# One transformer layer on one core: the split products stream their moving operand and their result from the last column to the first

## The chip, the cores and the metric

The kernel runs on one core of a Trainium2 chip. The metric is the device time of one execution in microseconds. Before the change the median of three runs is 1590.91 us, the lowest 1588.34 and the highest 1592.03. The profile shows one further execution of 1586.72 us, whose span from the first to the last instruction is 1585.0 us.

## The reference

The layer takes x of 512 tokens by 1024 in float32. Cut to what matters here:

```
h    = rms_norm(x)
proj = h @ w_in                       # 1024 x 3328
A, B, M = stick-breaking attention, gated recurrence, attention into 256 memory tokens
x    = x + concat(A, B, M) @ w_out    # 1024 x 1024
h2   = rms_norm(x)
q    = h2 @ w_query                   # 1024 x 2048, then the 16 best of 128 keys, twice, in 8 heads
act  = gelu(h2 . expert_u[idx])       # 16384 experts of 1024 numbers
x    = x + sum(gate * act * expert_v[idx])
```

All large products are float32 in the reference.

## The kernel before

The engines are TensorE (PE, with its weight load PEld), VectorE (DVE), ScalarE (ACT), GpSimd (POOL) and SyncE (SP). The order of the work is laid down by a planner: the stages are generators, the class `Pace` holds an estimated clock for each engine, and the class `Threads` always continues the stage whose estimated time is smallest. Each call goes through one recording helper, line 204, so nearly every row of the profile has the line L204, and groups are told apart by tiles.

A float32 product is made of three products in the type float32r. Each operand is split in a high part and a low part, and high by high, low by high and high by low are added up in one bank of PSUM. The helper `mm3` (line 417) issues these three. A stationary operand always is 128 by 128; the moving operand is 256, 384 or 512 columns wide, and each product has a weight load of its own.

The stages that call `mm3`, with the tile that the profile names as the result:

- `proj_t` (line 497): projections with tokens on partitions, 256 columns, tile `pt` in the input projection and the memory keys, `qp` in a part of the query projection (`query`, line 1037).
- `outproj` (line 961): the output projection, 256 columns, tile `op`.
- `query` (line 1101): the rest of the query projection, 384 columns, tile `qf`.
- `dense`: for three of the four blocks of 128 tokens every expert is computed. `u_mm` (line 1394) makes the 128 blocks of `expert_u`, with 24 products of 384 columns each, tile `ua`; `v_mm` (line 1469) makes the 128 blocks of `expert_v`, with 18 products of 512 columns each into six banks that stay open to the end, tile `pin`.

Not through `mm3` go the other part of the input projection (`proj_f`, line 484, tile `pf`, the same three products written out by hand), the recurrence (`hs` and others, plain float32), the attention scores (`sz`), and the sums of one-hot rows (`gsum`, line 1267, tile `gb`, float16, whose operands are read with a step of two elements).

The fourth block of tokens fetches its expert rows one by one with indirect DMAs of POOL, and VectorE multiplies them, beside `dense`. Results of PE are read by ACT or DVE in their usual order of columns; these reads are not in the diff.

Of the kernel before, what the change touches and what calls it, by code (L numbers as in the profile page):

```python
# [264 lines left out]
def tile_trunk_layer(ctx: ExitStack, tc: tile.TileContext, x, mem, w_in, w_kv, w_out, w_query,  # L265
# [43 lines left out]
    def f(ap):  # L309
        return ap.bitcast(F32)  # L310


    xs = [page([P, D], name="x") for _ in range(NT)]
    mt = [page([P, D], name="mem") for _ in range(2)]
# [100 lines left out]
            return (a, b), (c, d)  # L415

    def mm3(o, lh, ll, rh, rl, first, last):
        PE.matmul(o, lh, rh, start=first, stop=False)
        PE.matmul(o, lh, rl, start=False, stop=False)
        PE.matmul(o, ll, rh, start=False, stop=last)  # L420
# [76 lines left out]
    def proj_t(W, t, o, xh, xl):  # L497
        hi, lo = W
        for k in range(KD):
            a, c = t * P, t * P + P  # L500
            mm3(o, hsl(xh, k, a, c), hsl(xl, k, a, c), hi[k // 4][:, k % 4], lo[k // 4][:, k % 4],
                k == 0, k == KD - 1)
# [458 lines left out]
    def outproj(ts):  # L961
        yield f"mix{ts[0]}"
        xr, ob = {}, {}
        for c in range(4):
            hi, lo = ws.get()
            for t in ts:
                if th.later(f"mix{t}"):
                    yield f"mix{t}"
                if t not in xr:
                    xr[t] = page([P, D], name="xr")  # L970
                    SP.dma_start(xr[t], x[t * P:(t + 1) * P])
                if c % 2 == 0:
                    ob[t] = bank("op")
                mh, ml = mix[t]
                for k in range(KD):
                    mm3(ob[t][:, (c % 2) * 256:(c % 2) * 256 + 256], mh[:, k], ml[:, k],
                        hi[k // 4][:, k % 4], lo[k // 4][:, k % 4], k == 0, k == KD - 1)
                if c % 2:
                    yield "pe"
                    cs = slice((c // 2) * 512, (c // 2) * 512 + 512)  # L980
                    V.tensor_tensor(xr[t][:, cs], xr[t][:, cs], ob[t], op=OP.add)
                if c == 3:
                    th.add(norm2(t, xr[t]), at=pace.unit_v + ND2)
            yield "pe"
# [52 lines left out]
    def query(ts, todo):  # L1037
# [49 lines left out]
        for n, h in enumerate(todo):  # L1087
# [8 lines left out]
            if ts is DENSE and n >= QF:  # L1096
                for c in range(2):
                    b = bank("qf")
                    for k in range(KD):
                        w, lw = [x[k // 4][:, k % 4, c * P:(c + 1) * P] for x in W]  # L1100
                        mm3(b[:, :TD], w, lw, hsl(h2hi, k, 0, TD), hsl(h2lo, k, 0, TD), k == 0, k == KD - 1)
                    qT = t2([P, TD], name="qT")
                    A.activation(qT, b[:, :TD], AF.Copy)
                    if pend2:
                        tail2()
                    if pend:
                        tail()
                    elif len(pendf) > 1:
                        tailf()
                    pendf.append(qT)  # L1110
                    yield
                continue
# [555 lines left out]
```

## Time and profile before

| what | value |
|---|---|
| median of three runs | 1590.91 us |
| profiled execution | 1586.72 us |
| its span | 1585.0 us |
| PE busy | 1557.2 us, 98% |
| PEld busy | 1424.2 us, 90% |
| DVE busy | 1267.9 us, 80% |
| ACT busy | 749.5 us, 47% |
| POOL busy | 353.2 us, 22% |
| mean granted TensorE clock | 0.995 of 2.4 GHz |
| DMA | 422.72 MB, mean 267 GB/s |

A row of matmuls gives the length of each from its start to its modelled end. Matmuls are pipelined, so the next starts long before that end; what one costs in a dense stretch is the distance from start to start. Rows of a timeline give the start, then the length, both in us.

### The profile page before, as it was taken

The page shows a single profiled execution, that of the slowest core. Times are in us where ns is not written, and L with a number is a line of the kernel's source. Part 1 is how long each engine was busy: PE and PEld are TensorE (multiplying, and loading weights), DVE is VectorE, ACT ScalarE, POOL GpSimd, SP SyncE. Part 2 cuts the span into 40 slices and gives each one's busy share as a digit, 9 for nine tenths or more (in the row PEclk, how much of TensorE's full clock was granted, in tenths as well). Part 3 has the DMA queues.
Part 4 walks back from the last instruction along what each step waited for, and adds up shares of the span by engine and source line. Part 5 has one row for each costly group of instructions (what it writes and reads, how often), then busy time and mean ns, then how long its engine had stood idle before and what let it go on. Part 6 is the DMA issues. An engine that isn't in the chain of part 4 may idle for free.

```text
span 1585.0 us, 25696 instructions
## 1 busy us (share of the span) xinstructions
PE 1557.2 (98%) x9367; PEld 1424.2 (90%) x9367; DVE 1267.9 (80%) x2536; ACT 749.5 (47%) x1428; POOL 353.2 (22%) x340
## 2 busy tenths in 40 slices
PE   8999999989999999999999999999999999999998
PEld 6998988888999999999999999988888888888887
DVE  5475669786788888788877878768889888888886
ACT  6331268844443455666566755433333333333332
POOL 3000000000061212112211111134344444344430
PEclk9999999989999999999999999999999999999999
DMA  6322203353397878889879888899999999999991
GB/s 253 107 81 80 70 12 107 129 191 121 110 332 262 263 237 291 277 298 309 264 270 302 273 295 275 284 408 408 408 407 408 398 377 383 394 386 377 368 378 75
DMA packets 163951, 422.72 MB, mean 267 GB/s; under 512 B 13552, under 2 KB 62704, under 8 KB 163824
## 3 DMA queue, kind: packets, MB, share of 16 engines
q1 hardware_dynamic: 67824, 236.51, 40.9%
q0 software_dynamic: 36864, 134.23, 23.0%
q10 hardware_dynamic: 59136, 50.34, 9.9%
q8 instruction: 73, 1.20, 0.3%
q14 instruction: 54, 0.44, 0.1%
HBM read 366.50 MB, written 54.53 MB: 266 GB/s over the span
## 4 chain that ended last, share of the span: by engine, by line
PE 95%; DVE 2%; ACT 2%; DMA 0%; issue 0%; SPq 0%; ACTq 0%; DVEq 0%
PE ua L204 34%; PE pin L204 33%; PE pf L204 6%; PE pt L204 4%; PE qf L204 4%; PE gb L204 3%; PE op L204 3%; PE sz L204 2%; PE hs L204 2%; PE qp L204 1%; PE so L204 1%; PE qs L204 1%; DVE tka L204 1%; ACT se L204 1%; DMA w<-in_w_in_dram 0%; PE mo L204 0%
## 5 line engine op out<-in xcount | busy, mean ns | idle before, releaser
L204 DVE TENSOR_TENSOR xlo<-ex,xhi 128x1024 fp32r<-128x1024 f32 x256 | 312.5, 1221 | 99.3 <-issue 46.3
L204 POOL DMA_INDIRECT row<-in_u_rows_dram,eidx x128 | 157.8, 1233 | 924.1 <-DVE tka L204 424.5
L204 PE MATMUL ua<-h2hi,xhi 128*128 128x384 f32 x1024 | 349.1, 341 | 0.0
L204 PE MATMUL ua<-h2hi,xlo 128*128 128x384 f32 x1024 | 342.9, 335 | 0.0
L204 PE MATMUL ua<-h2lo,xhi 128*128 128x384 f32 x1024 | 342.6, 335 | 0.0
L204 ACT ACTIVATE whi<-w 128x384 fp32r<-128x384 f32 (+1 forms) x202 | 142.6, 720 | 372.9 <-DVE w L204 325.1
L204 PE MATMUL pin<-xhi,whi 128*128 128x512 f32 x768 | 299.6, 390 | 1.5 <-ACT whi L204 1.5
L204 PE MATMUL pin<-xlo,whi 128*128 128x512 f32 x768 | 299.6, 390 | 1.2 <-DVE xlo L204 1.2
L204 PE MATMUL pin<-xhi,wlo 128*128 128x512 f32 x768 | 299.3, 390 | 0.0
L204 ACT ACTIVATE xhi<-ex 128x1024 fp32r<-128x1024 f32 x256 | 268.7, 1051 | 25.4 <-ACT stg L204 8.3
L204 POOL DMA_INDIRECT row<-in_v_rows_dram,eidx x128 | 178.3, 1393 | 253.1 <-DVE w L204 129.5
L204 DVE TENSOR_TENSOR wlo<-w,whi 128x384 fp32r<-128x384 f32 (+1 forms) x200 | 156.2, 795 | 90.5 <-PE pin L204 50.1
L204 PEld LDWEIGHTS ua<-h2lo,xhi 128*128 128x128 f32 x1024 | 192.5, 188 | 0.0
L204 PEld LDWEIGHTS ua<-h2hi,xhi 128*128 128x128 f32 x1024 | 192.2, 188 | 0.2
L204 PEld LDWEIGHTS ua<-h2hi,xlo 128*128 128x128 f32 x1024 | 192.2, 188 | 0.0
L204 PEld LDWEIGHTS pin<-xhi,whi 128*128 128x128 f32 x768 | 144.4, 188 | 31.9 <-ACT whi L204 1.8
L204 PEld LDWEIGHTS pin<-xlo,whi 128*128 128x128 f32 x768 | 144.6, 188 | 31.7 <-DVE xlo L204 1.5
L204 PEld LDWEIGHTS pin<-xhi,wlo 128*128 128x128 f32 x768 | 144.6, 188 | 30.0
L204 DVE SCALAR_TENSOR_TENSOR xg<-row,rsb,xg 128x1024 f32<-128x1024 f32 x128 | 163.7, 1279 | 0.9
L204 DVE CUSTOM_DVE_ANT_0 row<-row,xr 128x1024 f32<-128x1024 f32 x128 | 155.0, 1216 | 4.3 <-DMA row<-in_u_rows_dram,eidx 4.3
L204 ACT ACTIVATE gel<-ua 128x384 f32<-128x384 f32 x128 | 62.8, 491 | 190.0 <-PE ua L204 188.3
L204 ACT ACTIVATE oh<-oh,gpg 128x128 f16<-128x128 f16 x256 | 84.3, 436 | 16.3 <-DVE rsb L204 3.8
(262 smaller groups left out, 2283.7 us busy)
## 6 DMA issues: line engine op xcount, KB each, us to landing
ex<-in_u_t_dram SPq DMA_DIRECT2D x128, 512.0 KB
ex<-in_v_rows_dram SPq DMA_DIRECT2D x128, 512.0 KB
gel<-gel ACTq DMA_DIRECT2D x64, 384.0 KB
gd<-stg ACTq DMA_DIRECT2D x48, 512.0 KB
G<-gd SPq DMA_DIRECT2D x48, 512.0 KB
gel<-gel SPq DMA_DIRECT2D x64, 384.0 KB
w<-in_w_query_dram SPq DMA_DIRECT2D x28, 512.0 KB
w<-in_w_in_dram SPq DMA_DIRECT2D x26, 512.0 KB
```

The costliest lines, as they stand in the source:

```text
L204: r = fn(*args, **kw)
```

## The change

A helper `back` turns an access pattern round in all its free dimensions: the offset moves to the last element, and each step changes its sign. `mm3` applies it to the result in PSUM and to both parts of the moving operand, so that column n of the operand still goes to column n of the result, in descending order of n. The stationary operands stay as they are. The diff in full:

```diff
@@ -309,6 +309,15 @@
     def f(ap):
         return ap.bitcast(F32)
 
+    def back(ap):
+
+        d = [list(x) for x in ap.ap]
+        off = ap.offset
+        for a in range(1, len(d)):
+            off += d[a][0] * (d[a][1] - 1)
+            d[a][0] = -d[a][0]
+        return type(ap)(ap.tensor, off, d)
+
@@ -415,6 +424,7 @@
             return (a, b), (c, d)
 
     def mm3(o, lh, ll, rh, rl, first, last):
+        o, rh, rl = back(o), back(rh), back(rl)
         PE.matmul(o, lh, rh, start=first, stop=False)
         PE.matmul(o, lh, rl, start=False, stop=False)
         PE.matmul(o, ll, rh, start=False, stop=last)
```

On every engine the same instructions stand in the same order. What differs is on PE alone: some matmuls carry other waits. The first place is in the middle of the blocks of `expert_u`, where each first product into a new bank, `ua`, follows the last product of the block before it:

```order
 L204 MATMUL ua_5711<-h2lo_4067,xhi_5594 128x384
 L204 MATMUL ua_5711<-h2hi_4066,xlo_5634 128x384
-L204 MATMUL ua_5753<-h2hi_4060,xhi_5632 128x384 [waits Activation_49]
+L204 MATMUL ua_5753<-h2hi_4060,xhi_5632 128x384 [waits PE_49,Activation_49]
 L204 MATMUL ua_5753<-h2lo_4061,xhi_5632 128x384
 L204 MATMUL ua_5753<-h2hi_4060,xlo_5671 128x384 [waits DVE_49]
```

Nothing moved; the first product of the bank also waits for an earlier matmul of PE. The second place is the start of the `expert_v` blocks, the first product into each of the banks 2 to 6 of `pin`:

```order
 L204 MATMUL pin_11811<-xhi_11726,wlo_11799 128x512
-L204 MATMUL pin_11812<-xhi_11726,whi_11797 128x512
+L204 MATMUL pin_11812<-xhi_11726,whi_11797 128x512 [waits PE_49]
 L204 MATMUL pin_11812<-xlo_11801,whi_11797 128x512
 L204 MATMUL pin_11812<-xhi_11726,wlo_11799 128x512
-L204 MATMUL pin_11813<-xhi_11726,whi_11797 128x512
+L204 MATMUL pin_11813<-xhi_11726,whi_11797 128x512 [waits PE_49]
```

Here too the order is kept, and the first product of each bank carries a wait for PE that it did not have. Over the whole program the waits of PE for PE are 204 before and 334 now.

## Rows read from the trace of the kernel before

**Rows 1.** The page's parts 1 and 2: busy time, and 40 slices.

```profile
span 1585.0 us, 25696 instructions
PE 1557.2 (98%) x9367; PEld 1424.2 (90%) x9367; DVE 1267.9 (80%) x2536; ACT 749.5 (47%) x1428; POOL 353.2 (22%) x340
...
PE   8999999989999999999999999999999999999998
...
PEclk9999999989999999999999999999999999999999
```

**Rows 2.** The chain that ended last: shares by engine, then by line.

```profile
PE 95%; DVE 2%; ACT 2%; DMA 0%; issue 0%; SPq 0%; ACTq 0%; DVEq 0%
PE ua L204 34%; PE pin L204 33%; PE pf L204 6%; PE pt L204 4%; PE qf L204 4%; PE gb L204 3%; PE op L204 3%; PE sz L204 2%; PE hs L204 2%; PE qp L204 1%; PE so L204 1%; PE qs L204 1%; DVE tka L204 1%; ACT se L204 1%; DMA w<-in_w_in_dram 0%; PE mo L204 0%
```

**Rows 3.** Waits of PE, longest and shortest of 13: total us, times, longest.

```profile
PE nt L204 <- DMA x<-in_x_dram: 4.5, 1, 4.5
...
PE pf L204 <- DVE hlo L204: 0.3, 1, 0.3
```

**Rows 4.** Groups of matmuls by shape: count, busy us, mean ns, idle before.

```profile
L204 PE MATMUL ua<-h2hi,xhi 128*128 128x384 f32 x1024 | 349.1, 341 | 0.0
...
L204 PE MATMUL pin<-xhi,wlo 128*128 128x512 f32 x768 | 299.3, 390 | 0.0
...
L204 PE MATMUL pt<-whi,hlo 128*128 128x256 f32 x160 | 45.3, 283 | 0.0
...
L204 PE MATMUL op<-whi,mxl 128*128 128x256 f32 x128 | 38.0, 297 | 0.1
...
L204 PE MATMUL qf<-h2lo,whi 128*128 128x384 f32 x112 | 37.5, 334 | 0.0
...
L204 PE MATMUL qp<-whi,h2g 128*128 128x256 f32 x128 | 24.9, 287 | 0.0
...
L204 PE MATMUL qp<-wlo,h2g 128*128 128x256 f32 x64 | 18.1, 282 | 0.0
...
L204 PE MATMUL pt<-whi,mhi 128*128 128x256 f32 x32 | 9.2, 288 | 0.0
...
L204 PE MATMUL qp<-wlo,h2hi 128*128 128x256 f32 x24 | 6.8, 282 | 0.0
```

**Rows 5.** The chain in order of time, two long pieces: start us, us.

```profile
467.87 83.21 PE ua L204 x480
...
1055.98 523.27 PE pin L204 x2300
```

**Rows 6.** Timeline of PE from 169.9 us: 256-column products, then plain float32.

```profile
169.92 0.28 PE L204 MATMUL pt<-whi,hhi 128*128 128x256 f32 x1
170.04 0.28 PE L204 MATMUL pt<-wlo,hhi 128*128 128x256 f32 x1
170.16 0.28 PE L204 MATMUL pt<-whi,hlo 128*128 128x256 f32 x1
170.28 1.95 PE L204 MATMUL hs<-fkq 128*128 128x128 f32 x16
171.98 0.36 PE L204 MATMUL pt<-whi,hhi 128*128 128x256 f32 x1
```

**Rows 7.** Timeline of PE from 700.8 us: the float16 products among those of `ua`.

```profile
700.78 0.34 PE L204 MATMUL ua<-h2hi,xlo 128*128 128x384 f32 x1
700.96 1.09 PE L204 MATMUL gb<-oh 128*128 128x128 f16 x16
701.86 0.42 PE L204 MATMUL ua<-h2hi,xhi 128*128 128x384 f32 x1
```

**Rows 8.** Two stretches: length, PE busy (count), PEclk, DMA share, GB/s.

```profile
470.00:551.00 81.00, 81.00 (x469) 1.00 0.80 264
1060.00:1560.00 500.00, 500.00 (x2207) 1.00 0.98 382
```

## The prediction

> **What bounds the kernel now.** I read the page's busy times first: PE is busy for 1557.2 of 1585.0 us, in nearly every one of the 40 slices, at the full granted clock [rows 1]. The chain of waits says the same in another way: 95% of what ended last is PE, two thirds of it the products of `ua` and `pin` alone [rows 2]. The list of PE's waits has 13 entries, the longest 4.5 us at the start and the shortest 0.3 us [rows 3]. So PE has no slack to give or to lose: whatever the change does to the distance between the starts of two split products comes out in the time, and what it does elsewhere must first cover PE to count.
>
> **How a product's time is made up.** The lengths of 280 to 390 ns in the groups [rows 4] are not what one costs, since the next starts before the modelled end. The starts tell: 480 products of `ua` take 83.21 us, 173.4 ns each at 384 columns; the piece of `pin` is 523.27 us [rows 5] for 2304 products (128 blocks of 18; the trace lacks four records), 227.1 ns each at 512 columns. The difference is 53.7 ns for 128 columns, 0.4195 ns a column, and what is left is a fixed 12.3 ns a product. The 256-column products fit: 0.12 us from start to start [rows 6] against 107.4 + 12.3 = 119.7 ns. So nearly all of the time is columns streamed at about 2.4 GHz, with a small fixed gap.
>
> **What the change touches.** The groups give the counts [rows 4]: `ua` 3 x 1024 of 384 columns, `pin` 3 x 768 of 512, `pt` 3 x 160 and 3 x 32 of 256, `op` 3 x 128 of 256, `qf` 3 x 112 of 384, `qp` 128 + 64 + 3 x 24 of 256. That is 6936 products with 1,179,648 + 1,179,648 + 147,456 + 98,304 + 129,024 + 67,584 = 2,801,664 columns. At 0.4195 ns and 12.3 ns they hold 1175 + 85 = 1260 us of PE, about 80% of the span. The projections `pf`, the recurrence and the one-hot sums keep their direction.
>
> **The terms.** Removed: nothing. Added: no instruction on any engine; the order of each engine is the same row for row. What changes is, first, the direction in which a column is read and written, and second, some waits of PE.
>
> The waits first. PE waits for PE in 334 places in place of 204. In each the awaited matmul stands at least seven products further up in PE's own order, at least 7 x 0.12 = 0.84 us earlier, and the longest record of a split product in these groups is 0.39 us; so it has ended, and the wait costs nothing. Queued behind such a wait is the whole rest of PE's work, so if that cover were gone (if the awaited matmul were the one just before) each would cost up to 0.39 us, 130 x 0.39 = 51 us. I take 0. DVE and ACT read results only after the last product of a group, so which column came first cannot matter to them.
>
> The direction is the whole question, and no row before shows a negative step. I bound it by the nearest rows.
>
> From above: the slowest streaming in this trace is the plain float32 of the recurrence, 16 records of 128 columns in 171.98 - 170.28 = 1.70 us [rows 6], 106 ns each or 0.830 ns a column, twice what the split products need. If a descending stream ran at that rate, it would add 0.830 - 0.4195 = 0.41 ns a column: 2,801,664 x 0.41 = 1150 us.
>
> From the side of the gap: the float16 products `gb` start 0.90 us / 16 = 56.3 ns apart [rows 7]; less 128 x 0.4195 = 53.7 this leaves 2.6 ns of gap, against 12.3. So a gap of PE is not one fixed figure but differs by 9.7 ns with the form of the operands. If the new direction took away or doubled that part: 6936 x 9.7 = 67 us either way.
>
> At zero: `gb` reads its moving operand with a step of two float16 elements, and still streams at 0.42 ns a column [rows 7]. So PE's read side does not need a step of one element to run at its full rate; a step of minus one, which touches the same words in the mirrored order, is nearer to that than to plain float32, which is slow for its type and not for its pattern. Each result still is one contiguous run of PSUM, and two consecutive columns are still neighbours. I take 0 for the rate and 0 for the gap, and keep +1150 and -67 as ends.
>
> The Trainium skill, in "PSUM — Partial Sum Buffer", section "Specifications (TRN2)", speaks against the change: its table says of the 8-byte lines "any non-contiguous AP slows matmuls significantly". Read strictly, a descending run is not a contiguous pattern, and the result would be the half rate of the first rival below; read by what lies in memory, the two columns of a line still follow each other, and the sum stays at 0. No row before writes PSUM in anything but ascending runs, so the trace cannot say which.
>
> The sum is 1586.7 us + 0 for an execution like the profiled one. The median of the runs shown lies 4.2 us above that execution, so the forecast is 1591 us.
>
> **The rivals.**
>
> A. The descending stream runs at half rate, because two columns no longer leave PE together. It decides from the first product in which PE takes 0.830 instead of 0.4195 ns a column: `ua` would go from 173 to some 331 ns, `pin` from 227 to some 437 ns. PE has nothing to hide this with [rows 1], so all 1150 us show: 1586.7 + 1150 + 4.2 = 2741 us. For it: the trace has work at half the column rate [rows 6], so PE has such a rate, and no row shows a result written in descending order at the full one. Against it: `gb` keeps the full rate with a read step that is not one [rows 7], though its result ascends. Chance 0.24.
>
> B. The rate holds, but each product pays more to begin, since its first column lies at the far end of the run: a gap doubled in the part that differs between `gb` and the split products, 9.7 ns, or 67 us on all 6936: 1586.7 + 67 + 4.2 = 1658 us. For it: the gap does differ by the form of operands [rows 5, 7]. Against it: nothing shows that it is made of address work. Anything between B and A, such as a charge for every few columns, I count here too. Chance 0.13.
>
> C. Faster: the gap of 12.3 ns shrinks to the 2.6 ns of `gb`. Not all 67 us could be had, as in the stretch of `pin` the DMA engines are already busy 0.98 of the time at 382 GB/s, while in that of `ua` it is 0.80 [rows 8]. Without `pin` there are 4632 products, 45 us: 1586.7 - 45 + 4.2 = 1546 us. For it: a gap of that size is not a law of PE [rows 7]. Against it: between two products the last column of one and the first of the next lie a whole run apart in both directions, so there is no distance that the mirror would change. Chance 0.13.
>
> D. That the change does not do what it says: the order of the columns would have to be undone between the program and the engine. Then the time is that of the forecast, and it is counted there.
>
> **How the numbers follow.** No change in the column rate and the gap, D included: 0.50. A 0.24, B 0.13, C 0.13. Within 0.2%, which is about what a measurement of this kernel can tell from no change (3 us; the three runs lie within 3.7 us), I put 0.47, as a few of the 130 new waits or a shift of the DMAs may push the likeliest case over that edge: 0.02 go to faster and 0.01 to slower. Faster then is 0.15, slower 0.38. The likeliest case has its own range of 1585 to 1598 us. For 8 times in 10 that is not enough, and neither is it with B: leaving out A's 0.24 alone is too much. So the range goes up to A at 2750 us, and leaves out C below: 1585 to 2750 us.
>
> **What would show it.** In the profile after, the piece of `pin` in the chain should stay at 523 us and that of 480 `ua` products at 83 us; `pf`, which keeps its direction, is the control and must stay at 227 ns from start to start whatever happens. Half rate would show as 437 and 331 ns beside an unchanged `pf`, the DMA share of the late stretch would fall to about half, and DVE's share of the span with it. Rival B or C would move the distances of 256, 384 and 512 columns by the same few ns. A wait that costs would show as a release of PE by PE in the list of waits, ahead of first products of `ua` only. The prediction is wrong if the distance per column, worked out from `ua` and `pin` as above, is not 0.42 ns, or if the fixed rest leaves 12 ns by more than one or two.

## The result, and the profile after

The changed kernel is slower by 1.6%: its median is 1615.53 us of four runs (1612.44 to 1616.15), against 1589.62 us of before in the same comparison. The ratio is 1.0157, with a 95% interval of 1.0141 to 1.0172. The profiled execution took 1615.93 us, with a span of 1614.2 us, 29.2 us more than the span of [rows 1].

The page after, the lines that answer to [rows 1]:

```profile
span 1614.2 us, 25730 instructions
PE 1586.3 (98%) x9367; PEld 1439.9 (89%) x9367; DVE 1269.1 (79%) x2536; ACT 749.4 (46%) x1428; POOL 357.3 (22%) x340
```

PE's busy time grew by 29.1 us, as much as the span. DVE and ACT worked about as long as before, POOL 4.1 us longer, and the weight loads (PEld), which run along with PE, 15.7 us longer. So the loss is on PE itself, which still holds 95% of the chain. The chain in order of time (start, length, what) shows on which products; of before, first, the two pieces that are not in the rows ahead:

```profile
58.30 8.63 PE pt L204 x72
...
413.44 8.32 PE qf L204 x48
```

And of after:

```profile
25.29 32.66 PE pf L204 x144
57.94 8.52 PE pt L204 x72
...
416.21 8.54 PE qf L204 x48
...
471.81 85.34 PE ua L204 x480
...
1071.54 536.95 PE pin L204 x2300
```

The control holds: `pf`, which was not turned, has 32.66 / 144 = 226.8 ns from start to start, to the hundredth as before. Of the turned ones each width went its own way:

| tile, columns | before, ns | after, ns | difference | products | together |
|---|---|---|---|---|---|
| `pin`, 512 | 523.27 / 2304 = 227.1 | 536.95 / 2304 = 233.1 | +5.9 | 2304 | +13.7 us |
| `ua`, 384 | 83.21 / 480 = 173.4 | 85.34 / 480 = 177.8 | +4.4 | 3072 | +13.6 us |
| `qf`, 384 | 8.32 / 48 = 173.3 | 8.54 / 48 = 177.9 | +4.6 | 336 | +1.5 us |
| `pt`, `op`, `qp`, 256 | 8.63 / 72 = 119.9 | 8.52 / 72 = 118.3 | -1.5 | 1224 | -1.9 us |

The sum is 26.9 of the 29.2 us (256 columns by `pt` for all three). Of the rest, 1.7 us lies in the attention scores, whose first products, `sz<-sq,sk`, were busy for 14.9 in place of 13.2 us, in a stretch (200 to 350 us) where the granted clock had a mean of 0.94 in place of 0.97. PE's list of waits has the same 13 entries as [rows 3], and none is a wait for PE.

### The profile page after: what moved, and what is told of

The parts are those of the page before. It is cut to its first block, busy times and chain, and to the rows that moved or that the text cites. A ratio compares the mean times of both kernels' runs of the same rounds, so it can differ in the third digit from the quotient of the medians.

```text
span 1614.2 us, 25730 instructions
## 1 busy us (share of the span) xinstructions
PE 1586.3 (98%) x9367; PEld 1439.9 (89%) x9367; DVE 1269.1 (79%) x2536; ACT 749.4 (46%) x1428; POOL 357.3 (22%) x340
## 4 chain that ended last, share of the span: by engine, by line
PE 95%; DVE 2%; ACT 2%; DMA 0%; issue 0%; SPq 0%; ACTq 0%; DVEq 0%
PE ua L204 34%; PE pin L204 33%; PE pf L204 5%; PE pt L204 4%; PE qf L204 4%; PE gb L204 3%; PE op L204 3%; PE sz L204 2%; PE hs L204 2%; PE qp L204 1%; PE so L204 1%; PE qs L204 1%; DVE tka L204 1%; ACT se L204 1%; DMA w<-in_w_in_dram 0%; PE mo L204 0%
## 5 line engine op out<-in xcount | busy, mean ns | idle before, releaser
L204 PE MATMUL ua<-h2hi,xhi 128*128 128x384 f32 x1024 | 355.6, 347 | 0.0
L204 PE MATMUL ua<-h2hi,xlo 128*128 128x384 f32 x1024 | 350.0, 342 | 0.0
L204 PE MATMUL ua<-h2lo,xhi 128*128 128x384 f32 x1024 | 348.5, 340 | 0.0
L204 PE MATMUL pin<-xhi,whi 128*128 128x512 f32 x768 | 305.5, 398 | 1.5 <-ACT whi L204 1.5
L204 PE MATMUL pin<-xlo,whi 128*128 128x512 f32 x768 | 305.5, 398 | 1.2 <-DVE xlo L204 1.2
L204 PE MATMUL pin<-xhi,wlo 128*128 128x512 f32 x768 | 305.4, 398 | 0.0
```

Source lines behind the costliest of these rows:

```text
L204: r = fn(*args, **kw)
```

## The experiments

Three theories stood at first. R: the descending read of the moving operand costs. W: the descending write of the result costs. N: other engines' traffic on the same memory costs, and the change only moves who meets whom. The width of 256, which became cheaper, spoke against any simple charge by the column.

**One half of the change alone.** In two kernels only `ua` and `pin` turn, and of them only the operand or only the result. The body of `mm3` where these two call it:

```diff
-        o, rh, rl = back(o), back(rh), back(rl)
+        rh, rl = back(rh), back(rl)        # read_only
+        o = back(o)                        # write_only
```

> Only the products of ua and pin, and of these only the moving operand descends; the result ascends, so it comes out mirrored, and the layer's output is not the reference's. Theory R: ua 178 and pin 233 ns as in the after kernel, the whole at about 1.017 of before. Theory W: 173.4 and 227.1 ns, ratio 1.000. Theory N with reads as the cause: as R; with writes as the cause: as W.

> Only the products of ua and pin, and of these only the result descends; the operand ascends, so the result is mirrored, and the layer's output is not the reference's. Theory W: ua 178 and pin 233 ns as in the after kernel, the whole at about 1.017 of before. Theory R: 173.4 and 227.1 ns, ratio 1.000. If neither read_only nor write_only shows it, the two directions cost only together.

Measured: read_only 1615.88 us, ratio 1.0171 (1.0153 to 1.0189); write_only 1588.49 us, ratio 1.0001 (0.9990 to 1.0012). The chain of read_only:

```profile
472.52 85.33 PE ua L204 x480
1072.24 539.61 PE pin L204 x2300
```

and of write_only, where both pieces are to the hundredth those of [rows 5]:

```profile
470.12 83.21 PE ua L204 x480
1058.35 523.27 PE pin L204 x2300
```

The whole loss is the read, and the write is free. The pair also settles the waits: write_only carries 311 waits of PE for PE (before 204, after 334) and is not slower, while read_only carries 204, as before, and is. The Trainium skill's sentence on PSUM ("PSUM — Partial Sum Buffer", "Specifications (TRN2)") therefore does not bite on a descending run; the measurement decides, and by it such a run costs nothing.

**The quiet stretch.** To tell R from N, `proj_f` was turned as well, which runs where the DMA engines are busy for a third of the time.

```diff
-            PE.matmul(b, hi[k // 4][:, k % 4, cs], hsl(hhi, k, 0, T), start=k == 0, stop=False)
+            PE.matmul(back(b), hi[k // 4][:, k % 4, cs], back(hsl(hhi, k, 0, T)), start=k == 0, stop=False)
...
```

> The after kernel with the 384 products of the input projection pf (512 columns, a quiet stretch, DMA share 0.31) turned round as well. Theory R or W (width decides): pf goes from 227 to about 233 ns from start to start, +2.3 us in all. Theory N (traffic decides, late stretches have a DMA share of 0.8 to 0.98): pf stays at 227 ns or falls a little, as the 256-column pt products of the same stretch did (119.9 to 118.3 ns).

Measured: 1616.9 us in one run. Its chain:

```profile
25.57 33.60 PE pf L204 x144
```

33.60 / 144 = 233.3 ns, the figure of `pin` in the busy stretch. N falls for `pf`: its 512 columns pay the same in the quiet stretch as those of `pin` in the busy one.

**PE alone.** All other work was left out but for the loads at the start and ACT's copy of each series' result: series of 48 products, each with its own weight load, one after the other, and what descends named by the tile.

```diff
+            down = mode == "down" or mode == "turn" and i % 2
+            if down or mode == "read":
+                r = back(r)
+            if down or mode == "write":
+                y = back(y)
+            PE.matmul(y, w, r, start=i == 0, stop=i == NP - 1)
```

> Only series of 48 products on PE, each with its own weight load, are left of the layer: the output is no layer's. Nothing else moves data meanwhile. Series differ in width (512, 384, 256, 128 columns of float32r; 512 of float16) and in what descends: nothing (up), moving operand and result (down), the operand alone (read), the result alone (write), or every second product (turn). Theory R (the descending read of SBUF costs): read and down show the after kernel's distances, about 233 ns at 512 and 178 ns at 384 columns, write and up about 227 and 173.4. Theory W (the descending write of PSUM costs): write and down at 233 and 178, read and up at 227 and 173.4. Theory N (the cost comes from other engines' traffic on the same memory): all modes within 1 ns of up, since nothing else runs. If the cost sits only where the direction changes, turn alone is dear. 256 columns descending: 1.5 ns below ascending by R or W if the width decides, equal to ascending by N.

The timeline of PE (start us, length us, what). A series' distance is the difference of two neighbouring starts over 48:

```profile
22.89 8.51 PE L76 MATMUL up_wide<-mv,wt 128*128 128x384 f32 x48
31.24 5.91 PE L76 MATMUL up_half<-mv,wt 128*128 128x256 f32 x48
36.99 5.92 PE L76 MATMUL up_rear<-mv,wt 128*128 128x256 f32 x48
...
59.31 8.70 PE L76 MATMUL down_wide<-mv,wt 128*128 128x384 f32 x48
67.84 5.84 PE L76 MATMUL down_half<-mv,wt 128*128 128x256 f32 x48
73.53 5.84 PE L76 MATMUL down_rear<-mv,wt 128*128 128x256 f32 x48
...
95.77 8.70 PE L76 MATMUL read_wide<-mv,wt 128*128 128x384 f32 x48
104.30 5.84 PE L76 MATMUL read_half<-mv,wt 128*128 128x256 f32 x48
...
131.96 8.51 PE L76 MATMUL write_wide<-mv,wt 128*128 128x384 f32 x48
140.31 5.91 PE L76 MATMUL write_half<-mv,wt 128*128 128x256 f32 x48
...
193.34 10.54 PE L76 MATMUL short_up<-mh,wh 128*128 128x512 f16 x48
203.72 10.52 PE L76 MATMUL short_down<-mh,wh 128*128 128x512 f16 x48
214.07 10.52 PE L76 MATMUL short_read<-mh,wh 128*128 128x512 f16 x48
```

At 384 columns up and write are 174.0 ns, down and read 177.7; at 256 columns 119.8 and 118.5. The kernel's numbers come out with next to nothing else running, so N is gone. In float16 (`short`), 512 columns take 216.3 ns up and 215.6 down: no cost at all. That is what my witness `gb`, a float16 row, could not show. Alternating directions (turn, not shown) gave 231.0 ns at 512 columns, between the 229.0 of write and the 234.4 of down in this run (not shown either).

**What of the read.** The next series kept the result ascending and changed the read: all widths, other steps, a stationary operand of 32 or 64 columns with its shorter load, and the two halves of "descending" taken apart. Numbers of float32r stand in groups of four, 16 bytes: lines reads the groups in descending order but each from front to back, inner the groups in ascending order but each from back to front.

```diff
+                if dims == "lines":
+                    r = type(r)(r.tensor, base + 4 * (lines - 1), [d[0], [-4, lines], [1, 4]])
+                else:
+                    r = type(r)(r.tensor, base + 3, [d[0], [4, lines], [-1, 4]])
```

> Again only series of 48 products on a quiet PE, result ascending throughout; the output is no layer's. Known so far: the descending read costs +5.4 ns at 512 columns, +3.7 at 384, -1.4 at 256, 0 at 128 in float32r and nothing in float16. Theory L (the moving read meets the read of the next weights, 188 ns long, in SBUF): with a stationary operand of 32 or 64 columns (shorter load) up and down move towards each other and towards N/2.4 + 3 ns (163 at 384, 216 at 512); a stationary operand read with a step of 8 changes the distances too; the penalty should grow with the width only as long as the load lasts. Theory S (the descending stream itself is slower in float32r, whatever the weights): the difference down - up stays +3.7 and +5.4 ns with 32 or 64 columns, and grows steadily from 192 to 512 columns by some 0.02 to 0.03 ns a column. Theory A (only the first line of four numbers is read awkwardly, as a descending run starts at its end): start offsets of 1, 2, 3 change down by a nanosecond or more and ascending likewise, offsets of 4 to 128 not. Order of lines against order within a line: if lines (-4, then 4 up) costs as down, it is the line order; if inner (4 up, then 4 down) does, it is the order within a line. A step of 0 reads one word only: if it falls to N/2.4 + 3 ns, the gap of float32r is reading.

The timeline again:

```profile
266.68 8.73 PE L92 MATMUL upoff_a<-mv,wt 128*128 128x384 f32 x48
275.25 8.70 PE L92 MATMUL downoff_a<-mv,wt 128*128 128x384 f32 x48
283.79 8.48 PE L92 MATMUL upoff_b<-mv,wt 128*128 128x384 f32 x48
...
419.17 7.96 PE L92 MATMUL still_g<-mv,wt 128*128 128x384 f32 x48
426.97 17.12 PE L92 MATMUL uptwo_g<-mv,wt 128*128 128x384 f32 x48
443.91 16.98 PE L92 MATMUL downtwo_g<-mv,wt 128*128 128x384 f32 x48
460.71 8.71 PE L92 MATMUL lines_g<-mv,wt 128*128 128x384 f32 x48
469.26 8.51 PE L92 MATMUL inner_g<-mv,wt 128*128 128x384 f32 x48
477.61 8.48 PE L92 MATMUL upslot_g<-mv,wt 128*128 128x384 f32 x48
...
604.29 8.49 PE L92 MATMUL upcols_sg<-mv,wt 128*32 128x384 f32 x48
612.62 8.59 PE L92 MATMUL downcols_sg<-mv,wt 128*32 128x384 f32 x48
621.05 11.28 PE L92 MATMUL upcols_sk<-mv,wt 128*32 128x512 f32 x48
```

- lines is 178.1 ns, inner 174.0: it is the order of the 16-byte groups that costs, not the order within one.
- With a step of 0, one word read again and again, 384 columns take 162.5 ns, as float16 does (162.5, in a series not shown). So the 11 ns that ascending float32r takes beyond that go with what is read. At 512 columns it is 11.3 ns (227.1 and 215.8, not shown), so the part is of nearly one size at these two widths. Against the line through the two, an estimate, ascending has 9 ns too much at 288 columns and 14 at 480 (not shown).
- With a step of two numbers the time doubles, to 352.9 ns, descending 350.0. The Trainium skill ("SBUF — State Buffer", "Specifications (TRN2)") asks for at least two hits on a 16-byte line for the full bandwidth; two numbers of a line are two hits, and here they give half, so for this operand, at a mean granted clock of 0.998 in this run, the measurement says that two are too few.
- With a stationary operand of 32 columns, whose load takes 108 ns in place of 188, descending still costs 2.1 ns at 384 columns, half of the 4.2 with 128. Theory L, which blamed the next weights' read, had the difference vanish along with the gap; the ascending distance stayed at 173.5 ns. At 512 columns ascending even rises, to 231.7 ns, and descending adds 1.5 to it in place of 6.4; at 256 the sign turns, 113.8 ns up and 117.7 down (all but the 231.7 not shown). So L as it was put fails, but the weight load has a part in what a direction costs, and which part stays open.
- The column at which the operand starts matters too. From column 1 ascending takes 178.5 ns and descending 177.9. Over nine starts from 1 to 128 ascending takes 173.1 to 178.5 ns and descending 176.7 to 180.0 (most not shown). Theory A, by which only starts inside a group matter, falls: 4 and 32 change ascending too, to 175.6 and 175.8. At multiples of 128, where the split products' operands start in their tiles, descending costs its 4 ns.
- The difference of down and up by width (not shown) goes +0.5, -0.2, -1.5, +2.0, 0, +2.1, +4.2, +4.1, +4.2, +3.3 and +6.4 ns from 192 to 512 columns in steps of 32. It is no steady charge per column; theory S in that form falls too.

**Other orders of the groups.** If the order of groups sets the time, other orders than these two must have times of their own, perhaps better ones.

```diff
+        for s, t in ((2, "two"), (4, "four"), (8, "eight"), (16, "sixteen"), (32, "thirty")):
+            series(f"comb{t}_{tag}", n, [[4, s], [4 * s, n // 4 // s], [1, 4]])
+        for s, t in ((2, "two"), (4, "four"), (8, "eight"), (16, "sixteen"), (32, "thirty")):
+            series(f"rake{t}_{tag}", n, [[4, n // 4 // s], [n // s, s], [1, 4]])
```

> Series of 48 products on a quiet PE again, float32r, 384 (g) and 512 (k) columns; the output is no layer's. Each series reads the same columns in groups of four ascending numbers, and only the order of the groups differs: comb (groups far apart in turn: first every group of a block of two, four, ... taken across the run), rake (two, four, ... parts of the run read in turn), flip (two, four, sixteen neighbouring groups descending, the blocks ascending), pair and ratwo (eight numbers at a time, two halves). Theory B (consecutive groups meet in the same part of SBUF, and any order has its own cost by address): some orders are cheaper than ascending, towards the 162.5 and 215.8 ns of the step of 0, others dearer than descending (177.7 and 233.5). Theory D (descending alone is dear, from group to group): flip of two lies halfway or above, flip of sixteen near 178 and 234, and comb and rake at 173 and 227 like ascending. Theory C (any jump that is not to the next higher group is dear): comb, rake and flip all lie at 178 and 234 or above. mir series (mirra, mircom, mirsix) also write in that order; if writes stay free they equal rake, comb of two and comb of sixteen.

Four neighbours of the timeline at 384 columns, then three that mix both directions:

```profile
22.76 8.51 PE L77 MATMUL up_g<-mv,wt 128*128 128x384 f32 x48
31.10 8.54 PE L77 MATMUL combtwo_g<-mv,wt 128*128 128x384 f32 x48
39.48 8.35 PE L77 MATMUL combfour_g<-mv,wt 128*128 128x384 f32 x48
47.67 8.92 PE L77 MATMUL combeight_g<-mv,wt 128*128 128x384 f32 x48
...
120.90 8.79 PE L77 MATMUL fliptwo_g<-mv,wt 128*128 128x384 f32 x48
129.53 9.76 PE L77 MATMUL flipfour_g<-mv,wt 128*128 128x384 f32 x48
139.12 8.70 PE L77 MATMUL flipsixteen_g<-mv,wt 128*128 128x384 f32 x48
```

That is 173.8, 174.6, 170.6 and 182.3 ns for up and the combs of two, four and eight (the start after that of eight, 56.42, is not shown), 179.8 and 199.8 for flips of two and four. Theory B holds: the order changes the price, to both sides of ascending, and descending is only one of the mildly bad ones. By what the price goes, B does not say and no run shows. Theories D and C fall with the flip of four, far above descending, and the comb of four, below ascending. The orders that also write so (mircom 174.6, as combtwo) add nothing.

**A version that beats both.** The comb of four, read and written, in the kernel before, for 384 and 512 columns, beside a second look at such orders:

```diff
+    def comb(ap):
+
+        n = ap.ap[1][1]
+        return type(ap)(ap.tensor, ap.offset, [list(ap.ap[0]), [4, 4], [16, n // 16], [1, 4]])
...
+        if o.ap[1][1] > 256:
+            o, rh, rl = comb(o), comb(rh), comb(rl)
```

> The kernel before, with the 384- and 512-column products (ua, pin, qf) reading and writing groups of four columns in the order 0, 4, 8, ... of every sixteenth column (steps 16, then 4), the order that gave 170.6 in place of 173.8 ns at 384 columns, and 226.2 and 223.5 in place of 227.3 ns at 512, in a quiet series. Theory B (each order of the lines has its own cost): ua and qf fall by 3 ns (3408 products, 10 us), pin by 1 to 4 ns (2304 products, 2 to 9 us), together 12 to 19 us, a ratio of 0.988 to 0.993. Theory C (any order but ascending is dear in the full kernel, beside other traffic): ua 178 and pin 233 ns or above, ratio 1.017 or above. If the small gains were noise of a single series: 1.000.

> Quiet series again, each twice (a and b), at 256, 384 and 512 columns; the output is no layer's. combfour should repeat at 170.6 and 223 to 226 ns if the order decides, and come out at 173 and 227 ns if the first figures were noise. downcomb (the same four combs, each descending) and backcomb (the combs themselves in descending turn): by theory B they cost what their addresses cost, neither bound to be dear; if descending alone is dear, downcomb lies 4 to 6 ns above combfour, as down does above up. eights, eightfour, sixtwo and sixfour take eight or sixteen numbers at a time over the same distances: near ascending, 173 and 227 ns, if only the next line counts.

comb_four took 1577.6 us, ratio 0.9907 (0.9886 to 0.9928). Its chain:

```profile
471.36 81.93 PE ua L204 x480
...
1048.73 521.61 PE pin L204 x2300
```

`ua` fell to 170.7 ns, as in the series; `pin` only to 226.4, where quiet series of the same order had between 223.5 and 226.3. In orders_two the second pass repeated the first within 0.5 ns in all but two of 24 series (by up to 2 ns at 256 columns); at 384 columns backcomb was best with 167.1 ns, at 256 and 512 columns eightfour, with 113.5 to 113.8 and 220.0.

The best of each width then went into the kernel, `pf` too (best_orders):

```diff
+        if n == 384:
+            return type(ap)(ap.tensor, ap.offset + 12, [list(ap.ap[0]), [-4, 4], [16, n // 16], [1, 4]])
+        return type(ap)(ap.tensor, ap.offset, [list(ap.ap[0]), [8, 4], [32, n // 32], [1, 8]])
```

> The kernel before, with all split products (pf as well) in the order that was cheapest for their width in the quiet series: 384 columns in groups of four, every fourth group in turn, the four turns descending (167.1 in place of 173.3 ns), 256 and 512 columns in groups of eight, every fourth group in turn (113.5 and 220.0 in place of 119.8 and 227.4 ns). Theory B (a product's time is set by the order in which the moving operand's groups are read, and by the address): 1224 products less 6 ns, 3408 less 6.2 ns, 2688 less 7.4 ns, together 48 us, ratio 0.970. In the stretch of pin the transfers already fill 0.98 of the DMA engines' time, so its 17 us may not all come: ratio up to 0.980. If the quiet figures do not carry over to operands at other addresses, as those of comb_four at 512 columns did only in part (226.4 ns against 223.9), 0.985 to 1.000.

Its median is 1578.25 us over six runs, against 1589.66 us of before, a ratio of 0.993 and not the 0.970 hoped for. The runs fall in two groups, 1555.89 and 1556.44 us, and four from 1577.56 to 1581.56; a ratio of 0.9859 (0.9806 to 0.9913), which leaves out the two longest, mixes both groups. The profile is of the longest run. In it the blocks of `ua` themselves come at two lengths:

```profile
25.55 31.68 PE pf L204 x144
...
462.25 83.20 PE ua L204 x480
...
562.90 8.05 PE ua L204 x48
...
625.50 8.37 PE ua L204 x48
...
1040.57 533.55 PE pin L204 x2300
```

That is 167.7 or 174.4 ns for the same order and the same operand. At 512 columns `pf` has 31.68 / 144 = 220.0 ns and `pin` 231.6, again in one order. Neither length changes inside an unbroken stretch: 480 products of `ua` hold 173.3 ns, while the weights come from one buffer after another, and `pin` holds its own to the end. It changes only where other products, mostly `gb`, run between two blocks of `ua`, and there at most breaks (not shown). Were `pin` at the 220.0 of `pf`, its 2304 products would take 27 us less, an estimate from these two rows; the two groups of runs lie some 22 us apart. No run of the shorter group was profiled, so that `pin` makes the groups is not shown.

mixed_orders therefore took the orders that had held in the kernel: groups of eight for 256 columns, the comb of four for 384 and for `pin`. By its edit `pf` stayed with the groups of eight, and not with the comb of which its expectation speaks.

> All split products with their groups of columns in the orders that held both in a quiet series and in the full kernel: 256 columns in eights (pt went from 119.9 to 113.5 ns in the kernel, op from 130.5 to 125.1), 384 and 512 columns, pf too, in combs of four (ua 170.7, pin 226.4 ns in the kernel). By theory B: 1224 products less 5 to 6 ns (7 us), 3408 less 2.7 (9 us), 2304 less 0.7 (2 us), pf 384 less 1 to 3 (1 us): 19 us, ratio 0.988. If the runs are as uneven as those of best_orders, 0.98 to 0.99 with a wide interval.

Measured: 1569.29 us, ratio 0.9866 (0.9844 to 0.9888), the lowest median of the three kernels. `pin` gave nothing to it in the profiled run (523.21 us, not shown, against 523.27 of [rows 5]); `ua` fell to 170.7 ns and `pf` to 220.0 (81.94 / 480 and 31.68 / 144, not shown).

The last series asked whether addresses cause the two lengths: the moving operand at six fixed bases, the stationary one at fixed blocks.

```diff
+            w = wt[j == 2 and not same][:, s * P:(s + 1) * P]
+            r = mv[j == 1][:, lo:lo + n]
```

> Quiet series of 48 products of 384 columns (512 in the k series); the moving operand now starts at one fixed column of its tile (0, 128, 256, 384, 512, 640 for a to f), and in the slot series the stationary operand is one fixed block. The output is no layer's. If the address decides with the order, down - up is not 4 ns at every base but differs, and the cheap backcomb is cheap (167 ns) at some bases and dear (174 to 176 ns, as in half of the ua blocks of best_orders) at others. If only the order decides, all bases agree within half a nanosecond. If the stationary operand's address matters, the slots differ among each other.

```profile
39.50 8.34 PE L74 MATMUL comb_a<-mv,wt 128*128 128x384 f32 x48
47.69 8.63 PE L74 MATMUL backcomb_a<-mv,wt 128*128 128x384 f32 x48
56.16 8.51 PE L74 MATMUL up_b<-mv,wt 128*128 128x384 f32 x48
...
232.18 8.69 PE L74 MATMUL downslot_ax<-mv,wt 128*128 128x384 f32 x48
240.70 8.16 PE L74 MATMUL backslot_ax<-mv,wt 128*128 128x384 f32 x48
248.71 8.49 PE L74 MATMUL upslot_ay<-mv,wt 128*128 128x384 f32 x48
```

All six bases agree within 0.2 ns, down at 177.5 to 177.7 everywhere, and the blocks within 0.5. But backcomb is 176.5 ns in the first part and 166.9 in the second, at the same base: there it follows comb and the weights go through eight blocks, here it follows down and the weights stand in one block. Eight blocks alone do not make it dear, since with them it took 167.1 ns in orders_two, after yet another order. So what ran just before is the likeliest reason, and it fits best_orders, where the length changes only at a break; no run changed it alone, and how it would act was not found. The base of the moving operand, as a multiple of 128 columns, is ruled out. At these six bases descending shows one level only.

## Why the prediction was right or wrong

The sign was left open, and the likeliest case, no change at 1591 us, did not happen; the time of 1615.5 us lies in the stated range, near its lower end, between the forecast and rival B. That it does is luck more than insight: the range was stretched up to A, half rate, and the small charge on the read that came true has no term in the sum.

- **What bounds the kernel**: right. PE has nothing to hide a longer product with, and 29.1 us more of PE are 29.2 us more of span.
- **The waits at 0**: right. The list of PE's waits has the entries of before, and write_only, with 311 waits of PE for PE, has the ratio 1.0001.
- **The write at 0**: right, by write_only and the quiet series.
- **The read at 0**: wrong, and this is the step that failed. I took `gb`, which reads float16 with a step of two, as the nearest row, and argued that PE does not need a step of one. float16 pays for no direction at all (216.3 and 215.6 ns), and float32r with that step of two takes twice its time (352.9 ns), so the row said nothing of float32r, whose 16-byte groups hold four numbers and not eight. In float32r the order of the groups moves the time: descending +5.9 ns at 512 columns, +4.4 at 384 and -1.5 at 256. Why these orders cost what they do stays open.
- **A fixed gap of 12.3 ns**: right in size at these widths, wrong as a gap. The step of 0 shows 162.5 ns at 384 columns and 215.8 at 512, so some 11 ns of each product go with the read. The sign of being wrong that was built on it did come: worked out the same way, `ua` and `pin` after have 0.432 ns a column and a rest of 12 ns. But that is no rate either, since it would make 256 columns dearer, and they became cheaper. Rivals B and C priced this part as something at a product's start. Their size, 9.7 ns a product, is near those 11 ns, but for another reason than the one given. "Anything between B and A" is where I counted small charges; the measured one lies below B, +27 us in place of +67, and differs by width, where B had the same few ns for all.
- **Rival A**, half rate: did not happen for a step of minus one. It is what a step of two numbers costs (352.9 ns).
- **Rival C**, faster, with its reason against it ("no distance that the mirror would change"): the direction asked for did not win, but the order can, by 1.3% in mixed_orders. Whether the DMA engines would have held `pin` back was never put to the test: its distance fell only to 226.4 ns, which a quiet series of the same order also showed (226.5, in addresses).

## What to carry to other kernels

When PE is the bound, look at the distance from start to start and compare it with the same shape read by a step of 0: the difference, 11 ns here, goes with the read of the moving operand, and part of it can be won by another order of the columns, without moving one instruction. Take the nearest row in the type as well as in the pattern: a float16 row cannot vouch for a float32r one. And try an order in the whole kernel before trusting its figure from a quiet series, since here one held (170.7 for 170.4 ns) and another did not (231.6 for 220.0, a figure that a later quiet series of the same order did not repeat either, with 230.6, in addresses, not shown).

## What the runs showed of the hardware that was not expected

The direction of a write to PSUM cost nothing (`ua` 83.21 us for 480 products, `pin` 523.27 for 2304, both ways), nor did writing in combs of two (174.6 ns with and without), while the order in which float32r is read from SBUF moves a product of 384 columns between 167 and 227 ns (the rake of sixteen, not shown). At 256 columns descending is cheaper than ascending, 118.5 against 119.8 ns. A stationary operand read with a step of eight numbers makes products of 256, 384 and 512 columns all cost about 240 ns (239.4, 247.9 and 247.7), and the records of its loads are 332 to 343 ns long in place of 188 (not shown), which points to the load as what sets the pace there. And the same products can run at two lengths, 166.9 or 176.5 ns in the quiet series, 220.0 or 231.6 at 512 columns in the kernel, and hold the one that they began with until something breaks the stretch.
